# Squares by ACT from natural tiles, S5 operators on VectorE alone, tables turned in small steps

## Chip, cores and metric

One core of one Trainium2 chip runs the whole program. The metric is the device time of one execution in microseconds, the median of several runs.

## What is computed

A two-layer decoder trunk on x of 512 tokens by 2048 channels, float32. Layer 0 normalises x, multiplies it by one wide weight matrix (`ab_w_in`), and runs gated linear attention and forgetting attention side by side; layer 1 normalises, projects, and runs a diagonal complex state-space layer (S5), a GLU and an output projection. Cut to what the change touches:

```
def rms_norm(x, g):
    y = x * rsqrt(mean(x * x, axis=-1) + EPS)
    return y * g

def layer_ab(x, norm_g, w_in, ...):
    h = rms_norm(x, norm_g)
    g_q, g_k, g_v, g_lr, g_gate, f_q, f_k, f_v, f_f, f_gate = split(h @ w_in)
    ...

def s5_ssm(u, lam_re, lam_im, log_step, b_re, b_im, c_re, c_im, d):
    # groups of 16 channels share 64 complex states:
    # x_t = Lbar x_{t-1} + Bbar u_t ; y_t = Re(C x_t) + D u_t
```

S5 is computed in chunks of 8 tokens. Its operators depend on the parameters alone: powers of Lbar times C (`wc`), B with its factor (`wb`), and the products of the two, the taps (`KD`, with D on the diagonal). The kernel builds them while the first stages of layer 0 run.

## The kernel before

**Stages.** The first stages multiply the normalised x by columns of `ab_w_in`. `proj_x` and `proj_w` go over 16 tiles of 128 rows, two per chunk, so 8 chunks make a stage: one value stage (`gv0`, 512 columns), three gate stages (350, 350 and 348 columns, accumulators `g_a`), two transposed gate stages (`fg_a`, 512 columns each), then the q projection (`gq_a`) and the rest. For each chunk SP's queue loads the raw weights (`wload`, L147 and following, tile `wr`, three buffers), ACT casts them (`wh`, L166), DVE takes the remainder (`wl`, L167; four buffers of each, so two chunks), and PE runs 24 matmuls (L173 to L175: wh by the rounded x, wl by the rounded x, wh by x's remainder). Four accumulators per stage are evacuated at its end; the next stage reuses them.

**The first stage.** x comes transposed (`xT`, tiles `x`), is multiplied by the norm's gain on ACT (`hT_h`, L249), and DVE takes the remainder (`hT_l`, L250). `square` (L280 to L288) squares each tile on ACT into one buffer, and GpSimd adds it to `sq1`; `rstd_of_columns` sums the columns with four matmuls by a column of ones (`ps_r1`), and GpSimd's power gives `r1`, which the evacuation of the value stage needs (L617).

**The S5 work** is a generator (`s5_all`), of which the stages take a step per chunk through `paced`: one per chunk in the first stage, then three per four chunks. `s5_parameters` computes the powers on DVE (tiles `es..`, `em..`, `sn`, `cs`, `pri`, `bri`), in program order. `turn` transposes them on PE and copies them on ACT to the tables `tabc` (32 copies, two halves) and `tabb` (4), L465. `s5_operators` then makes 16 blocks. In block b SP loads `pd` (256 KB, L510, three buffers, two blocks ahead); GpSimd copies its first part to `wc` (L516), DVE multiplies (`wc`, L487), GpSimd multiplies (`s5t`, L487), DVE adds (L308), and GpSimd stores `wc` (L520) and makes `wby` and `wb` (L524, L525). Two steps later `taps` runs eight small matmuls (`k`, L534), ACT copies to one of two `kst` tiles (L536), DVE adds D on the diagonal (two stt on 128x16, L305), and GpSimd stores it (`KD`, L540). `lay_out_taps` copies KD to `MD` inside DRAM on SP's queue (L499) as soon as that KD has landed.

**Order.** Each engine and queue runs its own list in order. The tile scheduler sets these lists from program order, priorities (`high_priority` for weight casts and evacuations) and its own estimate; `keep_in_program_order` pins an instruction. `wr`, `pd` and `MD` all stand in SP's one list. All DMAs started by GpSimd stand in GpSimd's list between its arithmetic.

Of the kernel before, what the change touches and what calls it, by code (L numbers as in the profile page):

```python
# [8 lines left out]
F32 = mybir.dt.float32  # L9
# [30 lines left out]
def tile_trunk(  # L40
# [41 lines left out]
    G.memset(mhalf, -0.5)  # L82
    ones = const.tile([P, 1], F32, name="ones")
    G.memset(ones, 1.0)

# [191 lines left out]
    mix = []  # L277
    sq1 = t2("sq1")

    def square(k):  # L280

        xk = xt[k // 4][:, k % 4]
        if k == 0:
            tc.keep_in_program_order(A.activation(sq1, xk, AF.Square))
        else:
            junk = ev(f"junk{k}")
            tc.keep_in_program_order(A.activation(junk, xk, AF.Square))
            G.tensor_tensor(sq1, sq1, junk, op=ALU.add)  # L288

# [26 lines left out]
    dT = const.tile([P, 2, NB], F32, name="dT")  # L316
    dmask = const.tile([P, CI], F32, name="dmask")

    def s5_parameters(pp):
# [146 lines left out]

        yield
        for half in range(2):
            sl = slice(half * 4, half * 4 + 4)
            turn(f"tabc{half}", pri[:, 1 + half * 4:5 + half * 4], tc_.rearrange("p b y g n -> p n b y g")[:, sl], (1.0, 1.0), (-1.0, 1.0))  # L470
            yield
        turn("tabb", bri[:, 0:1], tb_.unsqueeze(1), (1.0, -1.0), (-1.0, -1.0))
        ts(bi_, bi_, -1.0, ALU.mult)
# [3 lines left out]
        V.tensor_copy(l8i.rearrange("p (b g) -> p b g", g=GB), tc_[:, :, 1, :, 7])  # L477
        tt(dmask, ident[:, 0:16], ident[:, 32:48], ALU.add)
        tt(dmask, dmask, ident[:, 64:80], ALU.add)
        tt(dmask, dmask, ident[:, 96:112], ALU.add)  # L480


    def s5_mul(eng, o, b, pd, y):
# [3 lines left out]
        return eng.tensor_tensor(o, t, c, op=ALU.mult)  # L487

# [13 lines left out]
    def s5_operators():  # L502
        with tc.tile_pool(name="pp", bufs=1) as pp:
# [4 lines left out]
            def load(b):  # L508
                pd = pp.tile([P, 4, GB, CI], F32, tag="pd", name=f"pd{b}", bufs=3)
                SP.dma_start(pd, s5_bc[:, b])  # L510
                return pd

            def operands(b, pd):
                tm = pp.tile([P, GB, T, CI], F32, tag="tm", name=f"s5t{b}", bufs=2)
# [9 lines left out]
                G.tensor_tensor(wy, pd[:, 2:], tb_[:, b].unsqueeze(3).to_broadcast([P, 2, GB, CI]), op=ALU.mult)  # L524
                G.tensor_tensor(wb, wy[:, 0].unsqueeze(2).to_broadcast([P, GB, 2, CI]), wy[:, 1].unsqueeze(2).to_broadcast([P, GB, 2, CI]), op=ALU.add)  # L525
                return wc, wb

            def taps(b, wc, wb):
                ks = kst[b % 2]
                ps = pst(f"k{b}")  # L530
                for hb in range(2):
                    for g in range(4):
                        gg = g * 2 + hb
                        PE.matmul(ps[g * 32:g * 32 + 32, hb * P:(hb + 1) * P], wb[:, gg].rearrange("p n c -> p (n c)"),  # L534
                                  wc[:, gg, 0:8].rearrange("p n c -> p (n c)"), start=True, stop=True)
                A.copy(ks[:, :, P:], ps[:, :256].rearrange("p (h n) -> p h n", h=2))  # L536
                for hb in range(2):
                    k0 = ks[:, hb, P:P + CI]
                    stt(k0, dmask, dT[:, hb, b:b + 1], k0, ALU.mult, ALU.add)
                G.dma_start(KD[b].rearrange("y (g n) -> g y n", g=4), ks.rearrange("p h n -> p (h n)"))  # L540

            pds, ops = [load(0), load(1)], {}
            yield
            yield
            for b in range(NB + 2):
                if b >= 2:
                    taps(b - 2, *ops.pop(b - 2))
                if b < NB:
                    ops[b] = operands(b, pds.pop(0))
                if b + 2 < NB:  # L550
                    pds.append(load(b + 2))
                yield
# [31 lines left out]

    def rstd_of_columns():
        nonlocal r1
        ps = pst("ps_r1")
        for i in range(NT):
            tc.keep_in_program_order(PE.matmul(ps[:, i:i + 1], sq1[:, i * P:(i + 1) * P], ones, start=True, stop=True))
        t = small("r1_s", 4)  # L590
        V.tensor_copy(t, ps[:, :NT])
        r1 = const.tile([P, NT], F32, name="r1")
        V.tensor_copy(r1, rstd_from(t, D, 4, "r1_p"))
        V.tensor_scalar(r1h, r1, 0.5, None, op0=ALU.mult)
# [25 lines left out]

    tc_ = tb_ = None

    def s5_all():
        nonlocal tc_, tb_
        with tc.tile_pool(name="tab", bufs=1) as tab:
            tc_ = tab.tile([P, NB, 2, GB, T], F32, name="tabc")
            tb_ = tab.tile([P, NB, 2, GB], F32, name="tabb")
            with tc.tile_pool(name="np", bufs=1) as pp:
                ordered[0] = True
# [4 lines left out]
    def first_hook():  # L634
# [758 lines left out]
```

## Time and profile before

| | |
|---|---|
| median of three runs | 1732.05 us (1731.59 to 1736.32) |
| the profiled execution | 1734.72 us, its span 1733.0 us |
| PE busy | 1677.7 us, 97% |
| DVE busy | 950.1 us, 55% |
| ACT busy | 637.4 us, 37% |
| POOL busy | 311.1 us, 18% |
| granted clock of PE | 0.987 of full speed |

PE is TensorE's matmuls, PEld its weight loads, DVE VectorE, ACT ScalarE, POOL GpSimd, SP the sync engine, which only starts DMAs. The shares are averages over the whole span; the change touches stages that take about a sixth of it.

### The profile page before, as it was taken

The numbers are of one execution on the slowest core, as the hardware profiler recorded it, in microseconds if no ns is written. First come the engines' busy times: TensorE is split into PE (matmuls) and PEld (weight loads), VectorE is DVE, ScalarE is ACT, GpSimd is POOL, SyncE is SP. The second block draws the span as 40 slices with busy tenths as digits, with TensorE's granted clock in tenths as the row PEclk, the third lists the DMA queues.
The fourth block names the chain that finished last, engine by engine and source line by source line (L and its number), as shares of the span: only waits on it lengthen the run. The fifth ranks groups of instructions, "written<-read, shape, count | busy, mean of one in ns | idle before, by whom it ended". The sixth has DMA issues, their size and how long they took to land.

```text
span 1733.0 us, 25458 instructions
## 1 busy us (share of the span) xinstructions
PE 1677.7 (97%) x9849; PEld 1380.0 (80%) x9849; DVE 950.1 (55%) x1686; ACT 637.4 (37%) x1186; POOL 311.1 (18%) x454
## 2 busy tenths in 40 slices
PE   7988979999999999999999999998999999999998
PEld 5988757788888888888888878786888788888886
DVE  8747874538543343355565775886762654443333
ACT  5352223625422362255343222223334433332223
POOL 5036643207100000010011122211112200020000
PEclk9998999999999999999999999999999999999999
DMA  5236776332223332342565899754679633363333
GB/s 198 84 109 211 250 218 205 101 96 86 74 65 96 95 93 79 124 162 79 135 188 170 189 233 222 211 155 136 204 222 281 179 118 98 97 217 96 96 96 128
DMA packets 151033, 255.36 MB, mean 147 GB/s; under 512 B 34872, under 2 KB 57416, under 8 KB 150784
## 3 DMA queue, kind: packets, MB, share of 16 engines
q1 hardware_dynamic: 99440, 163.80, 31.1%
q0 software_dynamic: 31488, 79.43, 16.2%
q10 hardware_dynamic: 19984, 10.52, 2.2%
q8 instruction: 77, 1.26, 0.3%
q14 instruction: 44, 0.36, 0.1%
HBM read 218.45 MB, written 43.53 MB: 151 GB/s over the span
## 4 chain that ended last, share of the span: by engine, by line
PE 77%; DMA 11%; issue 6%; DVE 4%; POOL 1%; ACT 1%; SPq 0%; ACTq 0%; POOLq 0%; DVEq 0%
PE gl_a L173 3%; PE gl_a L175 3%; PE gl_a L174 3%; PE cg_a L173 3%; PE co_a L174 3%; PE co_a L175 3%; PE cg_a L174 3%; PE co_a L173 3%; PE cg_a L175 3%; DMA wr<-in_ab_w_in_dram 3%; PE u_a L173 2%; PE u_a L175 2%; PE u_a L174 2%; PE fq_a L173 2%; PE fq_a L175 2%
## 5 line engine op out<-in xcount | busy, mean ns | idle before, releaser
L167 DVE TENSOR_TENSOR wl<-wr,wh 128x512 fp32r<-128x512 f32 (+2 forms) x560 | 397.6, 724 | 584.1 <-ACT wh L166 356.9
L166 ACT CAST wh<-wr 128x512 fp32r<-128x512 f32 (+2 forms) x560 | 337.5, 609 | 850.9 <-PE u_a L174 126.4
L173 PE MATMUL gl_a<-z_h,wh 128*128 128x512 f32 x256 | 100.3, 392 | 3.1 <-DVE gt L1229 3.1
L173 PE MATMUL cg_a<-h_h,wh 128*128 128x512 f32 x256 | 102.9, 402 | 0.0
L173 PE MATMUL u_a<-h_h,wh 128*128 128x512 f32 x256 | 101.0, 395 | 1.6 <-DVE ut L1111 1.6
L175 PE MATMUL u_a<-h_h,wl 128*128 128x512 f32 x256 | 100.1, 391 | 1.3 <-DVE wl L167 1.3
L174 PE MATMUL cg_a<-h_l,wh 128*128 128x512 f32 x256 | 100.6, 393 | 0.0
L175 PE MATMUL gl_a<-z_h,wl 128*128 128x512 f32 x256 | 100.3, 392 | 0.0
L174 PE MATMUL gl_a<-z_l,wh 128*128 128x512 f32 x256 | 100.2, 392 | 0.0
L175 PE MATMUL cg_a<-h_h,wl 128*128 128x512 f32 x256 | 100.2, 391 | 0.0
L174 PE MATMUL co_a<-wl,fh 128*128 128x512 f32 x256 | 99.7, 389 | 0.2 <-DVE wl L167 0.2
L174 PE MATMUL u_a<-h_l,wh 128*128 128x512 f32 x256 | 99.8, 390 | 0.0
L173 PE MATMUL co_a<-wh,fh 128*128 128x512 f32 x256 | 99.6, 389 | 0.0
L175 PE MATMUL co_a<-wh,fl 128*128 128x512 f32 x256 | 99.6, 389 | 0.0
L173 PE MATMUL g_a<-wh,hT_h 128*128 128x350 f32 (+1 forms) x192 | 65.5, 341 | 6.4 <-DVE mix L567 5.1
L174 PE MATMUL g_a<-wl,hT_h 128*128 128x350 f32 (+1 forms) x192 | 64.7, 337 | 3.7 <-DVE wl L167 3.7
L173 PE MATMUL fg_a<-hT_h,wh 128*128 128x512 f32 x128 | 52.8, 413 | 13.9 <-DVE gT L579 8.7
L175 PE MATMUL g_a<-wh,hT_l 128*128 128x350 f32 (+1 forms) x192 | 64.2, 334 | 0.0
L173 PEld LDWEIGHTS gl_a<-z_h,wh 128*128 128x128 f32 x256 | 48.4, 189 | 13.9 <-issue 3.5
L173 PEld LDWEIGHTS u_a<-h_h,wh 128*128 128x128 f32 x256 | 48.1, 188 | 12.3 <-issue 2.0
L175 PEld LDWEIGHTS u_a<-h_h,wl 128*128 128x128 f32 x256 | 48.0, 188 | 12.2 <-DVE wl L167 2.2
L173 PEld LDWEIGHTS cg_a<-h_h,wh 128*128 128x128 f32 x256 | 48.4, 189 | 11.3
(388 smaller groups left out, 3866.3 us busy)
## 6 DMA issues: line engine op xcount, KB each, us to landing
wr<-in_ab_w_in_dram SPq DMA_DIRECT2D x95, 512.0 KB
wr<-in_c_w_in_dram SPq DMA_DIRECT2D x64, 512.0 KB
wr<-in_ab_w_out_dram SPq DMA_DIRECT2D x32, 512.0 KB
wr<-in_glu_w_dram SPq DMA_DIRECT2D x32, 512.0 KB
wr<-in_c_w_out_dram SPq DMA_DIRECT2D x32, 512.0 KB
WcD<-wc POOLq DMA_DIRECT2D x16, 576.0 KB, 7.2
wcl<-WcD POOLq DMA_DIRECT2D x16, 576.0 KB, 6.6
MD<-KD SPq DMA_DIRECT2D x16, 512.0 KB
```

The source lines that it names most:

```text
L166: A.copy(h[:, :ncol], raw[:, k, :ncol])
L167: split[k].tensor_tensor(l[:, :ncol], raw[:, k, :ncol], f32(h[:, :ncol]), op=ALU.subtract)
L173: PE.matmul(ps, ah, bh, start=first, stop=False)
L174: PE.matmul(ps, ah, bl, start=False, stop=False)
L175: PE.matmul(ps, al, bh, start=False, stop=last)
```

## The change

1. The squares no longer come from the transposed tiles. `load_sq` loads x a second time, untransposed, as 16 tiles of 128 tokens by 512 channels (256 KB each, on SP's queue, three per chunk); ACT squares each with a sum along the row (`accum_out`). `rstd_first` adds the four sums of each token on DVE. GpSimd's 15 additions, the matmuls by ones and `rstd_of_columns` go.
2. `turn` yields after each transposed tile, so that the turning is 9 steps, not 3; the pace in the gate stages and the transposed gate stages becomes one step per chunk.
3. In `s5_operators` the arithmetic of GpSimd goes to DVE (`s5t`, `wby`, `wb`) and ACT (the copy to `wc`). `pd` is loaded by GpSimd's queue, with four buffers and three blocks ahead; `s5t` has one buffer.
4. D on the diagonal is prepared once for all blocks (`dk`), so that a block needs one addition on 128x2x16.

```
-    def square(k):
-        xk = xt[k // 4][:, k % 4]
...
-            tc.keep_in_program_order(A.activation(junk, xk, AF.Square))
-            G.tensor_tensor(sq1, sq1, junk, op=ALU.add)
+    def load_sq(n):
+        t = t2(f"xs{n}")
+        tc.keep_in_program_order(SP.dma_start(t, x2d[n // 4 * P:(n // 4 + 1) * P, n % 4 * 512:(n % 4 + 1) * 512]))
+        xsq.append((n, t))
+    def square():
+        n, t = xsq.pop(0)
+        A.activation(t, t, AF.Square, accum_out=ss1[:, n // 4, n % 4:n % 4 + 1])
...
                     for y, sg in enumerate((even, odd)):
                         A.activation(dst[hs, k, :, y], pv[y * 64:y * 64 + 64, k], AF.Copy, scale=sg[half])
+                yield
...
             def load(b):
-                pd = pp.tile([P, 4, GB, CI], F32, tag="pd", name=f"pd{b}", bufs=3)
-                SP.dma_start(pd, s5_bc[:, b])
+                pd = pp.tile([P, 4, GB, CI], F32, tag="pd", name=f"pd{b}", bufs=4)
+                G.dma_start(pd, s5_bc[:, b])
...
-                G.tensor_copy(wc[:, :, 0], pd[:, 0])
-                tc.keep_in_program_order(s5_mul(V, wc[:, :, 1:9], b, pd, 0))
-                s5_mul(G, tm, b, pd, 1)
+                A.copy(wc[:, :, 0], pd[:, 0])
+                tc.keep_in_program_order(s5_mul(wc[:, :, 1:9], b, pd, 0))
+                s5_mul(tm, b, pd, 1)
                 tt(wc[:, :, 1:9], wc[:, :, 1:9], tm, ALU.add)
...
-                G.tensor_tensor(wy, ...)
-                G.tensor_tensor(wb, ...)
+                V.tensor_tensor(wy, ...)
+                V.tensor_tensor(wb, ...)
...
-                for hb in range(2):
-                    k0 = ks[:, hb, P:P + CI]
-                    stt(k0, dmask, dT[:, hb, b:b + 1], k0, ALU.mult, ALU.add)
+                k0 = ks[:, :, P:P + CI]
+                tt(k0, k0, dk[:, :, b], ALU.add)
...
-            pds, ops = [load(0), load(1)], {}
+            pds, ops = [load(b) for b in range(3)], {}
...
+                if b + 3 < NB:
+                    pds.append(load(b + 3))
                 if b >= 2:
                     taps(b - 2, *ops.pop(b - 2))
...
+        while xsq:
+            square()
         for k in range(3 * n, min(3 * n + 3, KT)):
-            square(k)
+            load_sq(k)
         if n == 6:
-            rstd_of_columns()
+            rstd_first()
...
-    s5_steps = paced(s5, 3, 4)
+    s5_steps = paced(s5, 1)
```

The order on the queues, at three places. First SP's queue in the first stage, before (`wr_317` is the sixth weight chunk, `x_97` to `x_100` are quarters of the transposed x):

```order
L157 DMA wr_175<-in_ab_w_in_dram 128x2x512
L157 DMA wr_238<-in_ab_w_in_dram 128x2x512
L106 DMA x_99<-in_xT_dram 128x4x512
L157 DMA wr_317<-in_ab_w_in_dram 128x2x512
L157 DMA wr_401<-in_ab_w_in_dram 128x2x512
L106 DMA x_100<-in_xT_dram 128x4x512
L157 DMA wr_471<-in_ab_w_in_dram 128x2x512
L157 DMA wr_671<-in_ab_w_in_dram 128x2x350
```

and after the change, where `wr_314` is the sixth chunk and `xs` are the new tiles for the squares:

```order
L155 DMA wr_172<-in_ab_w_in_dram 128x2x512
L155 DMA wr_235<-in_ab_w_in_dram 128x2x512
L104 DMA x_97<-in_xT_dram 128x4x512
L104 DMA x_98<-in_xT_dram 128x4x512
L282 DMA xs_182<-in_x_dram 128x512
L282 DMA xs_184<-in_x_dram 128x512
L282 DMA xs_186<-in_x_dram 128x512
L282 DMA xs_248<-in_x_dram 128x512
L282 DMA xs_250<-in_x_dram 128x512
L282 DMA xs_252<-in_x_dram 128x512
L155 DMA wr_314<-in_ab_w_in_dram 128x2x512
L282 DMA xs_327<-in_x_dram 128x512
```

Six loads of `xs` and the last quarter of x now stand ahead of the sixth weight chunk.

Second, ACT at the end of the second gate stage (`tg_2398` is the tanh that evacuates its accumulators, the casts of 348 columns belong to the third), before:

```order
L166 CAST wh_0_1347<-wr_1345 128x350
L166 CAST wh_1_1351<-wr_1345 128x350
L166 CAST wh_0_1423<-wr_1421 128x348
L166 CAST wh_1_1427<-wr_1421 128x348
L565 ACTIVATE tg_2398_1405<-g_a_1052,r1h 128x350
L565 ACTIVATE tg_2398_1408<-g_a_1053,r1h 128x350
L565 ACTIVATE tg_2398_1411<-g_a_1054,r1h 128x350
L166 CAST wh_0_1457<-wr_1455 128x348
L166 CAST wh_1_1461<-wr_1455 128x348
L565 ACTIVATE tg_2398_1414<-g_a_1055,r1h 128x350
L536 COPY kst_1175<-k_1379 128x2x128
```

and after the change:

```order
L164 CAST wh_1_1322<-wr_1316 128x350
L164 CAST wh_0_1368<-wr_1366 128x348
L164 CAST wh_1_1372<-wr_1366 128x348
L514 COPY wc_1403<-pd_1310 128x8x16
L514 COPY wc_1450<-pd_1312 128x8x16
L562 ACTIVATE tg_2398_1350<-g_a_1026,r1h 128x350
L514 COPY wc_1509<-pd_1314 128x8x16
L562 ACTIVATE tg_2398_1353<-g_a_1027,r1h 128x350
L562 ACTIVATE tg_2398_1356<-g_a_1028,r1h 128x350
L164 CAST wh_0_1415<-wr_1413 128x348
L164 CAST wh_1_1419<-wr_1413 128x348
L562 ACTIVATE tg_2398_1359<-g_a_1029,r1h 128x350
```

Three copies from `pd` to `wc` now stand before and between the first tanh, and so ahead of the casts of the third stage's next chunks.

Third, SP's queue in the transposed gate stages, before:

```order
L157 DMA wr_2019<-in_ab_w_in_dram 128x2x512
L510 DMA pd_1847<-in_s_bc_dram 128x512
L499 DMA MD<-KD 1024x1x128
L157 DMA wr_2079<-in_ab_w_in_dram 128x2x512
L510 DMA pd_1957<-in_s_bc_dram 128x512
L499 DMA MD<-KD 1024x1x128
L157 DMA wr_2113<-in_ab_w_in_dram 128x2x512
L157 DMA wr_2173<-in_ab_w_in_dram 128x2x512
L510 DMA pd_2017<-in_s_bc_dram 128x512
L499 DMA MD<-KD 1024x1x128
L157 DMA wr_2233<-in_ab_w_in_dram 128x2x512
```

and after the change:

```order
L497 DMA MD<-KD 1024x1x128
L155 DMA wr_1830<-in_ab_w_in_dram 128x2x512
L497 DMA MD<-KD 1024x1x128
L155 DMA wr_1889<-in_ab_w_in_dram 128x2x512
L497 DMA MD<-KD 1024x1x128
L155 DMA wr_1948<-in_ab_w_in_dram 128x2x512
L497 DMA MD<-KD 1024x1x128
L155 DMA wr_2007<-in_ab_w_in_dram 128x2x512
L497 DMA MD<-KD 1024x1x128
L155 DMA wr_2066<-in_ab_w_in_dram 128x2x512
L155 DMA wr_2125<-in_ab_w_in_dram 128x2x512
```

`pd` has left the queue; MD and the weight loads alternate.

## Rows read from the trace of the kernel before

**Rows 1.** The page, busy times of the whole execution.

```profile
PE 1677.7 (97%) x9849; PEld 1380.0 (80%) x9849; DVE 950.1 (55%) x1686; ACT 637.4 (37%) x1186; POOL 311.1 (18%) x454
```

**Rows 2.** Table by stage: busy us of PE, PEld, DVE, ACT, POOL; clock, DMA share, GB/s.

```profile
133.00:180.00 47.00, 41.44 (x309) 37.52 (x308) 38.02 (x43) 10.96 (x27) 29.93 (x32) 0.89 0.71 222
180.00:294.00 114.00, 100.10 (x534) 77.84 (x534) 75.41 (x87) 27.75 (x53) 55.80 (x85) 0.96 0.75 234
294.00:1733.00 1439.00, 1417.30 (x8412) 1160.69 (x8410) 747.20 (x1336) 531.98 (x977) 179.92 (x293) 1.00 0.48 139
```

**Rows 3.** Timeline of ACT (start us, us): casts, a gate stage and a 512-column stage.

```profile
81.70 0.97 ACT L166 CAST wh<-wr 128x350 fp32r<-128x350 f32 x2 [2.87 <-PE g_a L175]
...
287.29 1.14 ACT L166 CAST wh<-wr 128x512 fp32r<-128x512 f32 x2 [4.33 <-PE fg_a L175]
```

**Rows 4.** PE matmuls of four stages (min/median/max ns, first and last start); timeline at 133.

```profile
L173 PE MATMUL gv_a<-wh,hT_h x128: 387/389/796, 5.1 to 440.8; 128*128 128x512 f32 x128
...
L173 PE MATMUL g_a<-wh,hT_h x192: 316/323/629, 62.4 to 177.7; 128*128 128x350 f32 x128, 128*128 128x348 f32 x64
...
L173 PE MATMUL fg_a<-hT_h,wh x128: 389/389/767, 179.8 to 292.5; 128*128 128x512 f32 x128
...
L173 PE MATMUL gq_a<-hT_h,wh x64: 389/389/499, 293.6 to 342.2; 128*128 128x512 f32 x64
...
133.17 0.32 PE L175 MATMUL g_a<-wh,hT_l 128*128 128x350 f32 x1
```

**Rows 5.** Table by stretch as in rows 2, first stage.

```profile
10.00:20.00 10.00, 8.95 (x39) 7.08 (x39) 8.02 (x12) 8.97 (x17) 6.43 (x5) 1.00 0.91 329
...
40.00:50.00 10.00, 10.00 (x37) 8.00 (x37) 10.00 (x43) 3.01 (x5) 1.83 (x1) 0.81 0.13 37
```

**Rows 6.** DVE's timeline near 12 us, then costly groups of DVE and POOL before 62.

```profile
9.59 1.41 DVE L250 SCALAR_TENSOR_TENSOR hT_l<-x,cols,hT_h 128x512 fp32r<-128x512 f32 x2 [0.60 <-ACT hT_h L249]
...
14.21 3.26 DVE L250 SCALAR_TENSOR_TENSOR hT_l<-x,cols,hT_h 128x512 fp32r<-128x512 f32 x2 [1.52 <-ACT hT_h L249]
...
L250 DVE SCALAR_TENSOR_TENSOR hT_l<-x,cols,hT_h 128x512 fp32r<-128x512 f32 x16 | 14.6, 925 | 3.8 <-ACT hT_h L249 3.8
...
L308 DVE TENSOR_TENSOR emp<-emp,emr 128x64 f32<-128x64 f32 x7 | 1.5, 216 | 0.0
...
L288 POOL TENSOR_TENSOR sq<-sq,junk 128x512 f32<-128x512 f32 x15 | 22.7, 1516 | 20.3 <-ACT junk L287 19.5
```

**Rows 7.** Timeline of ACT between the first two gate stages.

```profile
99.22 3.28 ACT L465 ACTIVATE tabc<-tabc 64x128 f32<-64x128 f32 x8
```

**Rows 8.** Waits from 103 to 294 us: total, times, longest us.

```profile
ACT wh L166 <- DMA wr<-in_ab_w_in_dram: 61.2, 11, 11.0
...
POOL wby L524 <- DMA pd<-in_s_bc_dram: 42.7, 9, 9.8
...
SPq L499 <- DMA KD<-kst: 60.9, 9, 11.5
```

**Rows 9.** Timelines of SP's queue, POOL and ACT near 220 us.

```profile
214.28 5.57 SPq L157 DMA_DIRECT2D wr<-in_ab_w_in_dram  x1
219.94 0.52 SPq L510 DMA_DIRECT2D pd<-in_s_bc_dram  x1
...
226.46 1.15 POOL L524 TENSOR_TENSOR wby<-pd,tabb 128x256 f32<-128x256 f32 x1 [9.79 <-DMA pd<-in_s_bc_dram]
...
225.78 1.14 ACT L166 CAST wh<-wr 128x512 fp32r<-128x512 f32 x2 [10.23 <-DMA wr<-in_ab_w_in_dram]
```

**Rows 10.** DVE's products of pd; KD's issue and landing; POOL's loads of x.

```profile
L487 DVE TENSOR_TENSOR wc<-tabc,pd x16: 1210/1213/2957, 117.7 to 259.7; 128x1024 f32<-128x1024 f32 x16
...
L540 POOL DMA_DIRECT2D KD<-kst x16: 722/757/777, 139.9 to 277.8; - x16
...
DMA to landing us min/median/max: 6.1/7.0/9.6
...
x<-in_x_dram POOLq DMA_DIRECT2D x16, 256.0 KB, 4.0
```

More of the change, by code (lines that the diff above doesn't have):

```diff
@@ L82, in tile_trunk @@
     G.memset(mhalf, -0.5)
-    ones = const.tile([P, 1], F32, name="ones")
-    G.memset(ones, 1.0)
     idle = ev("idle")
@@ L277, in tile_trunk @@
     mix = []
-    sq1 = t2("sq1")
-    def square(k):
-        xk = xt[k // 4][:, k % 4]
[L283 to L286, printed above, removed]
-            tc.keep_in_program_order(A.activation(junk, xk, AF.Square))
-            G.tensor_tensor(sq1, sq1, junk, op=ALU.add)
+    ss1 = const.tile([P, NT, 4], F32, name="ss1")
+    xsq = []
+    def load_sq(n):
[5 more added lines that the diff above has]
+        A.activation(t, t, AF.Square, accum_out=ss1[:, n // 4, n % 4:n % 4 + 1])
     fb = const.tile([8, 1], F32, name="fb")
@@ L316, in tile_trunk @@
     dT = const.tile([P, 2, NB], F32, name="dT")
-    dmask = const.tile([P, CI], F32, name="dmask")
     def s5_parameters(pp):
@@ L469, in s5_parameters @@
             sl = slice(half * 4, half * 4 + 4)
-            turn(f"tabc{half}", pri[:, 1 + half * 4:5 + half * 4], tc_.rearrange("p b y g n -> p n b y g")[:, sl], (1.0, 1.0), (-1.0, 1.0))
-            yield
-        turn("tabb", bri[:, 0:1], tb_.unsqueeze(1), (1.0, -1.0), (-1.0, -1.0))
+            yield from turn(f"tabc{half}", pri[:, 1 + half * 4:5 + half * 4], tc_.rearrange("p b y g n -> p n b y g")[:, sl], (1.0, 1.0), (-1.0, 1.0))
+        yield from turn("tabb", bri[:, 0:1], tb_.unsqueeze(1), (1.0, -1.0), (-1.0, -1.0))
         ts(bi_, bi_, -1.0, ALU.mult)
@@ L477, in s5_parameters, with s5_mul @@
         V.tensor_copy(l8i.rearrange("p (b g) -> p b g", g=GB), tc_[:, :, 1, :, 7])
[L478 to L483, printed above, removed]
+        dmask = nt("dmask", CI)
+        V.tensor_reduce(dmask, ident.rearrange("p (j c) -> p c j", j=4)[:, :CI], axis=mybir.AxisListType.X, op=ALU.add)
+        tt(dk, dmask.unsqueeze(1).unsqueeze(1).to_broadcast([P, 2, NB, CI]), dT.unsqueeze(3).to_broadcast([P, 2, NB, CI]), ALU.mult)
+    def s5_mul(o, b, pd, y):
         t = tc_[:, b, y].unsqueeze(3).to_broadcast([P, GB, T, CI])
         c = pd[:, y].unsqueeze(2).to_broadcast([P, GB, T, CI])
-        return eng.tensor_tensor(o, t, c, op=ALU.mult)
+        return V.tensor_tensor(o, t, c, op=ALU.mult)
     WcD = dr.tile([NB, P, GB * 9 * CI], F32, name="WcD")
@@ L508, in load @@
             def load(b):
-                pd = pp.tile([P, 4, GB, CI], F32, tag="pd", name=f"pd{b}", bufs=3)
-                SP.dma_start(pd, s5_bc[:, b])
+                pd = pp.tile([P, 4, GB, CI], F32, tag="pd", name=f"pd{b}", bufs=4)
+                G.dma_start(pd, s5_bc[:, b])
                 return pd
             def operands(b, pd):
-                tm = pp.tile([P, GB, T, CI], F32, tag="tm", name=f"s5t{b}", bufs=2)
+                tm = pp.tile([P, GB, T, CI], F32, tag="tm", name=f"s5t{b}")
                 wc = pp.tile([P, GB, 9, CI], F32, tag="wc", name=f"wc{b}", bufs=3)
-                G.tensor_copy(wc[:, :, 0], pd[:, 0])
-                tc.keep_in_program_order(s5_mul(V, wc[:, :, 1:9], b, pd, 0))
-                s5_mul(G, tm, b, pd, 1)
+                A.copy(wc[:, :, 0], pd[:, 0])
+                tc.keep_in_program_order(s5_mul(wc[:, :, 1:9], b, pd, 0))
+                s5_mul(tm, b, pd, 1)
                 tt(wc[:, :, 1:9], wc[:, :, 1:9], tm, ALU.add)
@@ L523, in operands @@
                 wy = pp.tile([P, 2, GB, CI], F32, tag="wby", name=f"wby_{b}", bufs=2)
-                G.tensor_tensor(wy, pd[:, 2:], tb_[:, b].unsqueeze(3).to_broadcast([P, 2, GB, CI]), op=ALU.mult)
-                G.tensor_tensor(wb, wy[:, 0].unsqueeze(2).to_broadcast([P, GB, 2, CI]), wy[:, 1].unsqueeze(2).to_broadcast([P, GB, 2, CI]), op=ALU.add)
+                V.tensor_tensor(wy, pd[:, 2:], tb_[:, b].unsqueeze(3).to_broadcast([P, 2, GB, CI]), op=ALU.mult)
+                V.tensor_tensor(wb, wy[:, 0].unsqueeze(2).to_broadcast([P, GB, 2, CI]), wy[:, 1].unsqueeze(2).to_broadcast([P, GB, 2, CI]), op=ALU.add)
                 return wc, wb
@@ L549, in s5_operators @@
                     ops[b] = operands(b, pds.pop(0))
-                if b + 2 < NB:
-                    pds.append(load(b + 2))
                 yield
@@ L583, in evac_gateT, with rstd_first @@
         return f
-    def rstd_of_columns():
+    def rstd_first():
         nonlocal r1
[L587 to L593, printed above, removed]
+        r1 = token_rstd(ss1, "r1")
         V.tensor_scalar(r1h, r1, 0.5, None, op0=ALU.mult)
@@ L619, in evac_gv @@
         return f
-    tc_ = tb_ = None
+    tc_ = tb_ = dk = None
     def s5_all():
-        nonlocal tc_, tb_
+        nonlocal tc_, tb_, dk
         with tc.tile_pool(name="tab", bufs=1) as tab:
@@ L627, in s5_all @@
             tb_ = tab.tile([P, NB, 2, GB], F32, name="tabb")
+            dk = tab.tile([P, 2, NB, CI], F32, name="dk")
             with tc.tile_pool(name="np", bufs=1) as pp:
```

## The prediction

> **What bounds the kernel now.** I read the page's busy times first [rows 1]: TensorE (PE) is busy 97% of the span, so little can be won, and the question is where. The table by stage answers it [rows 2]: from 294 us to the end PE is busy 1417.3 of 1439 us at a granted clock of 1.00, before that it is not, and the clock is lower. The whole change lies before 294 us, and behind it the orders of the engines are the same, so what the first stages win or lose is carried to the end.
>
> How much can be lost there follows from pitches. ACT casts a chunk when PE has done another, and where only PE holds it, busy and idle add up to PE's pitch: 0.97 + 2.87 = 3.84 us in a gate stage, 1.14 + 4.33 = 5.47 us in a 512-column stage [rows 3]. The first PE instruction of each stage [rows 4] gives what each took: the first value stage (8 chunks) 57.3 us against 43.8, the three gate stages (24) 117.4 against 92.2, the two transposed gate stages (16) 113.8 against 87.5. The last matmul of the second gate stage [rows 4] puts its end at 133.5, so gate stages 1 and 2 lost 9.7 us and the third 15.6. Lost in all: 13.5 + 9.7 + 15.6 + 26.3 = 65 us. That is the ceiling.
>
> Why each is lost. **First stage:** PE is behind, and VectorE (DVE) is the engine without a gap: from 40 to 50 us it is busy 10 of 10 us, while PE's clock is granted at 0.81 on average, a mix of the 2.4 and 1.2 GHz levels after PE's waits just before [rows 5]. DVE is slow because GpSimd adds squares: two hT_l take 1.41 us before GpSimd starts and 3.26 during its first additions [rows 6]. **Gate stages 1 and 2:** ScalarE (ACT) runs the copies of the turned tables in runs between the tanh of the evacuation (one of the four in [rows 7]), and PE, whose accumulators wait for those, idles. **Third gate stage and after:** ACT waits 61.2 us for weights (wr), GpSimd 42.7 us for pd, SP's queue 60.9 us for KD to land [rows 8]. The timelines show a ring: SP lays out MD only when a KD has landed, and the weight load behind it goes at 214.28, the pd behind that at 219.94; GpSimd stands 9.79 us until that pd is there, at 226.46, and only then issues its next KD, for which the next MD, weights and pd wait; ACT meanwhile waits 10.23 us for the weights [rows 9].
>
> **The change, part by part.**
> *A, squares.* Removed: 15 additions on GpSimd, 22.7 us [rows 6], and the four small ps_r1 matmuls. Against the undisturbed 0.70 the 16 hT_l of 925 ns hold 3.6 us too much, and wl and the small steps are stretched alike. The 16 squares stay on ACT. Added: 16 loads of 256 KB on SP's queue, 4.2 MB or 12.7 us at the 329 GB/s of the second 10 us, into a stage whose DMA share falls to 0.13 [rows 5]. Six of them and 2 MB of x now stand ahead of the sixth weight chunk; from 13 us on that is 3.6 MB, 11 us, so it lands near 26 to 28 us, and an unstalled PE needs it at 33. In the new order DVE runs 36 small steps in one piece before the wl of that chunk, 36 of 216 ns [rows 6], less than 8 us; I charge 3 us of PE waits to it and 1.5 to the late r1 (two last loads, two squares, the reduction, GpSimd's power), and 1.6 remain from the first two chunks. 13.5 - 6.1 gives **-7 us**.
> *B, tables.* The 16 copies of a half still stand together on ACT, but between two casts, away from the tanh: 16 x 0.41 + 0.97 = 7.5 us [rows 7] against two chunks of 7.68 until the cast is needed, with its wl about 0.9 us late. Twice that is 1.8 in place of 9.7: **-8 us**.
> *C, third gate stage.* New: in the order of ACT two copies wc<-pd stand ahead of the first tanh of the second gate stage, and on DVE the first s5t stands ahead of one wl. pd can only start when LbD has landed and kst is cleared. pd has no row on GpSimd's queue; the nearest are x, a load of the same 256 KB there, with 4.0 us, and KD, a store of 256 KB, with up to 9.6 [rows 10]; a pd already there would cost nothing. I take x's 4 and count the queue in the new order from the start of the last table: a wait of 2.3 us, plus 1.2 at the lower clock, 3.5; the ends are 0 and 9. DVE's part of a block becomes 3 x 1.21 [rows 10], 2 x 0.42 for wy and wb (256 columns, estimated between 0.22 for 64 and 1.21 for 1024), 0.22 for the tap [rows 6]: 4.7 us. Five blocks (23.5), 15 wl and four mix (some 0.5 each) stand ahead of the last wl of this stage, 33 us against 30.7 - 2 of PE: 4.4 late. The two kst buffers need a KD landed two chunks later: 3 us to its issue and 7.0 to landing (6.1 to 9.6 [rows 10]) against 2 x 4.4 here, for the few blocks of this stage about 3. So 30.7 + 10.9 against 46.3: **-5 us**. GpSimd's arithmetic goes, and with it DVE's stretched rows.
> *D, transposed gates.* pd no longer passes SP, so KD follows its block. KD is issued about 3 us after its matmuls, lands 8 later, MD and wr follow, wr lands 10 later (214.28 to the cast at 225.78 is 11.5 [rows 9]), cast and wl take 2.5: 23.5 us, and in the new order five chunks, 27.4 us, lie between. It fits narrowly. DVE needs 4.7 + 1.3 = 6.0 us per chunk while blocks remain (ten chunks), 0.5 above 5.47: 5.3; 7 more for late transfers and the two evacuations. 87.5 + 12.3 against 113.8: **-14 us**.
> The wc copies that move to ACT, where casts fill 1.14 of 5.47 us, I cost at nothing while pd is there first; if it is not, see the slower rival. GpSimd's three issues per block, pd's now among them, take some 0.75 each of 6 us.
>
> For the move of pd the Trainium skill speaks against a gain: DMA: Bandwidth & Descriptors, "Issuing engines are not separate DMA queues", says all queues run on the same 16 engines and that another issuer only saves issue time. By it D would lose its 14 us and the sum be 20, or 1712, close to the first rival below. The rows disagree: pd's issue takes 0.52 us on SP, but it stood behind a weight load that took 5.57 to go and an MD that waited for KD, and GpSimd paid 9.79 us for it [rows 9].
>
> **Sum:** 7 + 8 + 5 + 14 = 34 us. The profiled execution took 1734.7 us and gives 1700.7; the median of the three runs is 2.7 us lower, 1732.05, and gives **1698 us**.
>
> **Rivals.**
> *The 16 DMA engines become the bound.* From 133 to 294 us they are busy 0.71 x 47 + 0.75 x 114 = 119 us [rows 2]. The same transfers in my 141 us mean a share of 0.84; the best 10 us hold 0.91 [rows 5], the two stages now 0.71 and 0.75. If 0.77 is the most that holds for long, C and D end at 154 us in place of 160: with A and B a gain of 21, **1711 us**. Against it: much of today's idle share is the ring. Chance 0.22.
> *A or B fails* (the sixth weight chunk comes late behind the loads of squares; or the 16 copies in one piece stall PE as they do now, so that the small steps are none): 7 or 8 us less, **1706**. Chance 0.05.
> *All fits better:* DVE and KD hide behind PE, gain 46 to 55, **1682**. Chance 0.07.
> *Slower: ACT inherits the wait for pd.* GpSimd waits 4.7 us for pd on average (42.7 over 9 waits) and feeds no cast; ACT does. If each of 16 blocks held ACT for 7 us, 3.3 above the slack of 5.47 - 1.14 - 0.65, C and D would end at 118 (pitches) + 23 + 53 = 194 us in place of 160: with A and B **1751 us**. It decides from 6 us per block. For it: pd on GpSimd's queue stands behind WcD and KD, which wait for DVE. Against it: pd is issued three blocks, some 16 us, ahead. Chance 0.04.
> The Trainium skill bears on this rival: SBUF — State Buffer, "Summary: rules for kernel authors", advises the SP or ACT queue for a load under DVE work, since descriptors made on GpSimd starve in some of DVE's modes. KD's issue, 722 to 777 ns over 16 [rows 10], shows no such starving beside DVE's work.
> *No change* (half of each term, and the rest eaten by such waits): 1732, chance 0.02.
>
> **How the numbers follow.** Forecast (gain 24 to 46) 0.60, and the rivals as above. A measurement here tells 0.3%, 5.2 us, from no change. Faster 0.92 (forecast, DMA bound, A or B, all fits, less 0.02 for what I have not seen), same 0.03, slower 0.05. The range takes in the DMA rival to a gain of 12 and most of the better case: 1684 to 1720.
>
> **What would show it.** gate stages starting near 55 us, the third near 118 and the first q projection (gq_a) near 260; no GpSimd arithmetic from 10 to 250 us except one power; hT_l at 0.70 to 0.75 us throughout; no GpSimd wait for pd, SP's wait for KD well under 60.9 us, ACT's for wr well under 61.2; DVE near full and DMA share above 0.8 from 120 to 230 us; ACT and DVE waiting once for pd near 118 us. Wrong: ACT's wait for wr still above 50 us (DMA bound, or the ring through MD lives on without pd), or ACT waiting for pd block by block.

## The result, and the profile after

The changed kernel takes 1707.53 us (median of four runs, 1705.76 to 1711.91), the kernel before 1734.18 beside it: a ratio of 0.9835 with a 95% interval of 0.9805 to 0.9865. It is faster by 26.7 us where 34 were forecast, and lies in the range. The profiled execution has a span of 1704.2 us, against 1733.0.

The page's busy times of the changed kernel, for [rows 1]:

```profile
PE 1667.2 (98%) x9841; PEld 1374.0 (81%) x9841; DVE 920.9 (54%) x1717; ACT 643.0 (38%) x1218; POOL 224.0 (13%) x390
```

Its table by stretch and stage, with the columns of [rows 2]:

```profile
10.00:20.00 10.00, 10.00 (x45) 8.28 (x45) 8.06 (x18) 5.90 (x10) 0.00 (x0) 1.00 1.05 390
40.00:50.00 10.00, 10.00 (x46) 8.09 (x44) 4.00 (x19) 4.58 (x12) 1.05 (x1) 1.00 0.61 199
50.00:114.30 64.30, 64.03 (x398) 62.71 (x397) 30.02 (x79) 34.20 (x79) 4.06 (x7) 1.00 0.35 107
114.30:155.60 41.30, 35.66 (x290) 32.54 (x289) 34.16 (x57) 13.14 (x33) 9.51 (x16) 0.99 0.77 242
155.60:265.10 109.50, 101.73 (x549) 79.28 (x549) 72.51 (x111) 29.96 (x61) 31.15 (x76) 0.94 0.79 253
265.10:1704.00 1438.90, 1417.31 (x8415) 1161.39 (x8412) 747.90 (x1337) 532.68 (x978) 173.96 (x276) 1.00 0.48 139
```

The last row is the check that all of it lies ahead: 1438.9 us, where [rows 2] has 1439.0. The first row (10 to 20 us) now has PE without a gap. The third gate stage and the transposed gates are the two with idle PE. Their idle time, span less PE's busy time, is 5.6 and 7.8 us. The third gate stage of the kernel before, cut at the same landmarks, shows as much idle time (5.5 us), but a lower granted clock:

```profile
133.50:179.80 46.30, 40.76 (x304) 37.05 (x304) 37.48 (x43) 10.31 (x25) 29.23 (x31) 0.89 0.70 222
```

The first matmuls of the four stages, for [rows 4]:

```profile
L171 PE MATMUL gv_a<-wh,hT_h x128: 389/389/796, 5.1 to 412.3; 128*128 128x512 f32 x128
...
L171 PE MATMUL g_a<-wh,hT_h x192: 316/322/431, 50.0 to 150.7; 128*128 128x350 f32 x128, 128*128 128x348 f32 x64
...
L171 PE MATMUL fg_a<-hT_h,wh x128: 389/389/796, 155.6 to 264.0; 128*128 128x512 f32 x128
...
L171 PE MATMUL gq_a<-hT_h,wh x64: 389/389/499, 265.1 to 313.7; 128*128 128x512 f32 x64
```

The gate stages start at 50.0, the transposed gates at 155.6, the q projection at 265.1, 28.5 us earlier than before.

The waits from 100 to 265.1 us (total, times, longest), for [rows 8], first of the engines (a selection):

```profile
ACT wh L164 <- DMA wr<-in_ab_w_in_dram: 37.3, 9, 9.5
...
ACT wc L514 <- DMA WcD<-wc: 14.8, 5, 4.2
...
ACT wc L514 <- DMA pd<-in_s_bc_dram: 2.7, 3, 1.9
...
DVE s5t L485 <- DMA pd<-in_s_bc_dram: 1.8, 1, 1.8
```

and of SP's queue:

```profile
SPq L497 <- DMA KD<-kst: 9.8, 4, 8.0
```

SP's wait for KD fell from 60.9 to 9.8 us. GpSimd's 42.7 us for pd are gone, since it no longer reads pd; ACT and VectorE wait 4.5 us for it in its place. ACT still waits 37.3 us for weights, where it was 61.2, and the experiments below are mostly about that row.

### The profile page after: what moved, and what is told of

It reads as the page before. It is cut to its first block, busy times and chain, and to the rows that moved or that the text cites. A ratio compares the mean times of both kernels' runs of the same rounds, so it can differ in the third digit from the quotient of the medians.

```text
span 1704.2 us, 25406 instructions
## 1 busy us (share of the span) xinstructions
PE 1667.2 (98%) x9841; PEld 1374.0 (81%) x9841; DVE 920.9 (54%) x1717; ACT 643.0 (38%) x1218; POOL 224.0 (13%) x390
## 4 chain that ended last, share of the span: by engine, by line
PE 84%; issue 6%; DMA 5%; DVE 2%; POOL 1%; ACT 1%; POOLq 0%; ACTq 0%; DVEq 0%; SPq 0%
PE gl_a L171 3%; PE gl_a L173 3%; PE gl_a L172 3%; PE u_a L171 3%; PE u_a L173 3%; PE u_a L172 3%; PE co_a L172 3%; PE co_a L173 3%; PE co_a L171 3%; PE cg_a L171 3%; PE cg_a L172 3%; PE cg_a L173 3%; PE fq_a L171 2%; PE fq_a L173 2%; PE oa_a L171 2%
## 5 line engine op out<-in xcount | busy, mean ns | idle before, releaser
L165 DVE TENSOR_TENSOR wl<-wr,wh 128x512 fp32r<-128x512 f32 (+2 forms) x560 | 373.7, 681 | 593.9 <-ACT wh L164 357.0
L171 PEld LDWEIGHTS gl_a<-z_h,wh 128*128 128x128 f32 x256 | 48.5, 189 | 14.3 <-issue 4.3
L171 PEld LDWEIGHTS u_a<-h_h,wh 128*128 128x128 f32 x256 | 48.0, 188 | 12.3 <-issue 2.0
```

Source lines behind the costliest of these rows:

```text
L165: split[k].tensor_tensor(l[:, :ncol], raw[:, k, :ncol], f32(h[:, :ncol]), op=ALU.subtract)
L171: PE.matmul(ps, ah, bh, start=first, stop=False)
```

## The experiments

Each run is read by its stages, from the first matmul of one to that of the next (gate stages 1 and 2: to the end of the last matmul with 350 columns). These landmarks come from the one profiled execution of each kernel, and repeat within some 1.6 us where the code is the same (the first stage of the kernels with the new squares takes 44.0 to 45.6). The whole time repeats less well: in layer 1, whose code no run here changes, the stretch from the first u_a to the first cg_a matmul took 194.4 us before, 193.4 after the change and up to 201.4 in the other runs. A gain at the q projection is therefore not yet a gain of the median, and both are given where both were measured.

| kernel | first stage | gates 1, 2 | gate 3 | transposed gates | q starts at |
|---|---|---|---|---|---|
| before | 57.3 | 71.1 | 46.3 | 113.8 | 293.6 |
| before + squares | 45.0 | 71.9 | 45.5 | 112.0 | 279.4 |
| before + turning, pace 1 | 56.4 | 64.5 | 49.2 | 127.0 | 302.1 |
| before + arithmetic moved | 57.6 | 70.0 | 44.5 | 117.9 | 295.1 |
| before, MD later | 57.2 | 71.3 | 43.1 | 101.7 | 278.5 |
| **changed** | 44.9 | 64.3 | 41.3 | 109.5 | 265.1 |
| changed, pd on SP | 44.0 | 64.3 | 41.2 | 105.7 | 260.3 |
| changed, arithmetic on GpSimd | 44.5 | 64.3 | 47.8 | 112.0 | 273.8 |
| changed, MD later | 44.6 | 64.3 | 39.7 | 97.0 | 250.8 |
| changed, MD on GpSimd | 44.4 | 64.3 | 40.1 | 122.6 | 276.5 |
| changed, MD on GpSimd, behind | 45.6 | 64.3 | 41.2 | 100.8 | 257.0 |
| changed, MD on SP, behind | 44.7 | 64.3 | 41.6 | 108.2 | 264.0 |
| MD later + copies of x on SP | 44.4 | 64.3 | 39.5 | 115.9 | 269.2 |
| changed, MD later, blocks pinned | 45.2 | 64.3 | 33.3 | 98.2 | 246.2 |

Six of the kernels were run once only, and are read by their stages; no run has the fourth part, D on the diagonal, by itself. The single times are 1706.62 us (pd on SP), 1723.11 (arithmetic on GpSimd), 1721.73 and 1702.55 (MD on GpSimd, and behind), 1708.33 (MD on SP, behind) and 1726.50 (copies of x).

### One part at a time, in the kernel before

**Squares alone.** The edit is the first piece of the diff, with `load_sq`, `square`, `rstd_first` and the hook.

> The kernel before with the squares alone (loads of untransposed x, ACT's sums along the row, no additions on GpSimd); the S5 work as before. Theory (GpSimd's additions slowed VectorE in the first stage, and nothing else of the change acts there): the gate stages start near 50 us as in the changed kernel, not at 62.4, hT_l falls to about 0.7 us, and the 12 us are kept to the end: about 1722. Rival (the gain of the first stage is given back, because the blocks then meet the same ring earlier): the gate stages start near 50, but the q projection starts less than 6 us earlier than 293.6, and the time is above 1728.

1727.61 us, ratio 0.995 (0.9932 to 0.9968). The first stage takes 45.0 us, as in the changed kernel, and the q projection starts 14.2 us earlier: the gain is kept up to there, and the rival falls. The median time is 9.1 us below that of the kernel before beside it (1736.71), where 12 were expected. The profiled execution has the lowest of the ten times (1723.61), so its landmarks flatter the part somewhat. The ring lives on beside it (SP waits 59.1 us for KD).

**Turning and pace alone.**

```
-            turn(f"tabc{half}", ...)
-            yield
+            yield from turn(f"tabc{half}", ...)
...
-    s5_steps = paced(s5, 3, 4)
+    s5_steps = paced(s5, 1)
```

> The kernel before with the turning in nine steps and the pace of one step per chunk alone. Theory (ACT's runs of copies delayed the tanh at the ends of the stages): gate stages 1 and 2 take about 64 us in place of 71, and the time falls by about 7 to 1727. Rival (a faster pace only drives the ring of KD, MD and weights harder): the first two gate stages are shorter, but the third and the transposed gate stages together are longer by as much, and the time stays within 3 us of the kernel before.

1747.27 us, ratio 1.0052 (1.0032 to 1.0072): slower. The first two gate stages fall to 64.5 us, as the theory said, but the third and the transposed gates take 16.1 us more. The rival was right that they get longer, and the loss is larger than it said. Its reason does not show in the waits, though: SP waits less for KD than before (49.7 us for 60.9) and ACT less for weights (36.7 for 61.2). What grew is ACT's wait for one of the two kst buffers, that is, for an older KD to land; casts stand behind that copy on ACT's list. Before, from 100 to 300 us:

```profile
ACT kst L536 <- DMA KD<-kst: 15.1, 5, 3.9
```

and with the turning in steps and the pace of one:

```profile
ACT kst L536 <- DMA KD<-kst: 45.8, 11, 10.1
```

In the changed kernel it is 3.1 us. Alone, the part does not pay. The edit has two halves, and no run separates the steps of the turning from the pace.

**Arithmetic alone**, VectorE's and ACT's part of `operands`, with pd as before (the last run, after those below):

> The kernel before with the S5 operators' arithmetic moved to VectorE and ACT alone (pd stays on SP with three buffers and two blocks ahead, squares, turning and pace as before). Theory formed from the runs so far (the link of the ring that mattered is KD's place in GpSimd's list behind arithmetic that waits for pd): SP's wait for KD falls below 20 us from 60.9, third gate stage and transposed gates together fall from 160.4 us to 150 or less, the time by 8 to 14. Rival (it needs pd on its own queue as well, as the prediction had it): KD waits stay over 40 us, gain under 4.

1741.79 us, ratio 1.0036 (1.002 to 1.0051): my theory fell. The waits of this kernel from 100 to 300 us, VectorE's for pd:

```profile
DVE wby L524 <- DMA pd<-in_s_bc_dram: 38.4, 9, 5.3
```

and SP's queue for KD:

```profile
SPq L499 <- DMA KD<-kst: 70.1, 11, 8.4
```

What GpSimd waited for pd, VectorE now waits, nearly microsecond for microsecond (42.7 and 38.4), and VectorE feeds the weights too. In this kernel, the arithmetic without an earlier pd is worth nothing.

### Undoing one part of the changed kernel

```
-                G.dma_start(pd, s5_bc[:, b])
+                SP.dma_start(pd, s5_bc[:, b])
```

> The changed kernel with pd loaded by SP's queue again (four buffers and three blocks ahead stay, the arithmetic stays on VectorE and ACT). Theory of the prediction (what helped from the third gate stage on is that pd no longer passes SP, where it stood behind MD and weights): the ring is back, SP waits for KD more than 30 us in place of 9.8, and the q projection starts after 274 us in place of 265.1. Rival (what helped is that the arithmetic left GpSimd; pd three blocks ahead is early enough on either queue): the q projection starts within 3 us of 265.

The q projection starts at 260.3, SP waits 10.3 us for KD: no ring, and the theory of the prediction falls. The rival's 3 us are missed too, on the good side: the start is 4.8 us earlier than in the changed kernel. Once the load goes out three blocks ahead into four buffers, GpSimd's queue is no better for pd than SP's. ACT waits 23.5 us for pd in this run, and yet no stage is longer than in the changed kernel.

The arithmetic back on GpSimd (`G.tensor_copy`, `s5_mul(G, ...)`, `G.tensor_tensor` for wby and wb, two s5t buffers):

> The changed kernel with the S5 operators' arithmetic back on GpSimd and VectorE as before (s5t with two buffers), pd on GpSimd's queue three blocks ahead. Theory (pd's own queue was what helped): the q projection starts within 4 us of 265.1. Rival (the arithmetic on GpSimd stood between the transfers that its list starts and slowed VectorE's rows, so that it was the bound at a pace of one step per chunk): VectorE's products take well over 1.21 us on average, the transposed gates take over 118 us, the q projection starts after 274.

273.8, 8.7 us later, 6.5 of them in the third gate stage; SP waits 22.4 us for KD and ACT 54.4 for weights. Where the arithmetic stands matters, given an early pd. VectorE's products explain a part of it at most:

```profile
L485 DVE TENSOR_TENSOR wc<-tabc,pd 128x1024 f32<-128x1024 f32 x16 | 22.7, 1420 | 1.6 <-DMA pd<-in_s_bc_dram 1.6
```

Their mean is 1420 ns for 1218 in the changed kernel, 3.2 us over all 16. Their median is 1213 ns, as in [rows 10]: a few are slow, not all.

### The copies of the taps (MD)

`lay_out_taps` stands in the program much later, in the forgetting attention's k projection. The scheduler pulls the copies forward on SP's list to the place where each KD may be ready. One line keeps them back, in the kernel before and in the changed one (the first copy then starts at 457.1 us in place of 147.9, and at 429.1 in place of 137.9, some 300 us later and not the 200 that the expectations name):

```
-            SP.dma_start(MD[b]..., ...)
+            tc.keep_in_program_order(SP.dma_start(MD[b]..., ...))
```

> The kernel before with the copies of the taps (MD) pinned where the program has them, in the k projection of the forgetting attention some 200 us later, and nothing else changed; only SP's list differs. Theory of the ring (the wait of SP for KD, 60.9 us, held weights and pd): SP's wait for KD is gone before 294 us, ACT's wait for weights falls below 25 us from 61.2, and third gate stage and transposed gate stages together fall by 15 to 25 us: 1710 to 1719. Rival (the 16 DMA engines or GpSimd's arithmetic are the bound): less than 8 us, above 1726.

> The changed kernel with the copies of the taps (MD) pinned where the program has them, some 200 us later; only SP's list differs. Theory (what the transposed gates still lose, 22 us, is weights that land 10 to 14 us after their issue because the DMA engines are full at a share of 0.86, and MD is a good part of that load): the share falls below 0.75, ACT's wait for weights from 120 to 265 us falls from 37 to under 15, the transposed gates take about 95 us, and the time falls by 12 to 18: about 1692. Rival 1 (VectorE's 6 us per chunk bound it): share falls, VectorE is busy near 100%, the transposed gates take over 103 us, gain under 6. Rival 2 (ACT's copies to wc, which wait for the store WcD, hold the casts): ACT waits 12.9 us for WcD as now, gain under 6.

In the kernel before, this line alone brings 15.1 us at the q projection (293.6 to 278.5). The median time falls by 10.2 us, to 1726.55 (ratio 0.9946, 0.9923 to 0.9969), short of the 1710 to 1719 that were expected; here too the profiled execution has the lowest of ten times (1718.42). No wait for weights is left there, and GpSimd's wait for pd falls to 8.2 us. In the changed kernel it brings 14.3 us (265.1 to 250.8; 1697.02 us, ratio to before 0.9771, 0.9733 to 0.9809). The transposed gates of that version:

```profile
153.80:250.80 97.00, 96.25 (x548) 75.31 (x548) 72.17 (x111) 31.32 (x61) 30.63 (x76) 1.00 0.68 207
```

PE is busy 96.25 of 97.0 us at a clock of 1.00, VectorE 72. So VectorE is no bound, and ACT's wait for WcD (24.9 us in this run, more than in the changed kernel) costs nothing. Most of what PE does in the 9.5 us above the pitch of 87.5 is the taps, per block one group of eight small matmuls, which stand as 16 records in the trace, here in the changed kernel's timeline:

```profile
176.15 0.39 PE L173 MATMUL fg_a<-hT_h,wl 128*128 128x512 f32 x1
176.54 0.64 PE L532 MATMUL k<-wc,wb 128*32 128x128 f32 x16
177.11 0.50 PE L171 MATMUL fg_a<-hT_h,wh 128*128 128x512 f32 x1
```

From the last matmul ahead to the first behind it is 0.96 us, where 0.23 is the step: some 0.7 us per block, and ten blocks (160 of the 548 records) fall into this stage: 7 us.

Three causes for the late weights remained: MD's bytes, SP's waits for KD, or the copies on SP's queue by themselves. MD on GpSimd's queue keeps the bytes in the stage:

```
-            SP.dma_start(MD[b]..., ...)
+            G.dma_start(MD[b]..., ...)
...
                     taps(b - 2, *ops.pop(b - 2))
+                if b >= 4:
+                    next(laid)
```

> The changed kernel with MD copied by GpSimd's queue, two blocks behind the store of KD, in the same stages; SP's list is then weights alone. It keeps MD's bytes in the stage and takes its place in SP's list away. Theory of the bytes (full DMA engines make the weights late): DMA share near 0.8, ACT's waits for weights from 120 to 265 us over 25 us, the transposed gates 105 to 110 us. Theory of the list (SP's wait for KD and MD's turn ahead of the weights made them late): ACT's waits for weights under 10 us, the transposed gates 97 to 100 us as with MD moved away, the q projection near 252.

This try made a ring of its own and settles little:

```profile
POOL MD L497 <- DMA KD<-kst: 87.0, 15, 9.8
```

GpSimd stood for KD. Still, ACT had no wait for weights at all. So once more, with the copies pinned and begun at block 5 (`b >= 5`, `keep_in_program_order`); and, in another kernel, the same on SP's queue:

> MD on GpSimd's queue once more, now pinned five blocks behind the operators (three behind the store of KD), so that GpSimd no longer stands for KD, which took 87 us of its list in the first try. SP's list is weights alone, MD's bytes stay in the stage. Theory of the bytes: DMA share 0.78 to 0.85, ACT waits over 20 us for weights, the transposed gates take over 105 us. Theory of SP's list: no wait for weights, the transposed gates 97 to 101 us, the q projection at 251 to 255.

> MD on SP's queue between the weights as in the changed kernel, but each copy pinned three blocks behind its KD, so that SP has no KD to wait for; bytes and number of starts on SP as in the changed kernel. If SP's waits for KD (9.8 us there) made the weights late: no wait for KD, ACT's waits for weights fall from 37 us to under 12, the transposed gates take under 101 us. If the bytes, or MD's transfer ahead of the weights on the same queue, did it: the transposed gates take 105 to 110 us as in the changed kernel.

On GpSimd's queue the transposed gates take 100.8 us, with no wait for weights and the DMA engines fuller than in this stage of any other run:

```profile
156.20:210.00 53.80, 52.51 (x323) 40.06 (x324) 48.49 (x73) 15.31 (x36) 24.39 (x32) 0.97 0.97 317
```

A share of 0.97 at 317 GB/s, and the weights are in time. The theory of the bytes falls. One thing besides the queue changed, however: on SP's queue a copy of 512 KB goes out as 1024 packets of 512 bytes, on GpSimd's as 128 of 4 KB and some tiny ones. Over the transposed gates SP's queue (hardware) and GpSimd's (software) moved, in packets, MB and share of the engines, in the changed kernel

```profile
q1 hardware_dynamic: 19505, 17.01, 49.4%
q0 software_dynamic: 5186, 10.64, 28.9%
```

and with MD on GpSimd, behind,

```profile
q0 software_dynamic: 9404, 19.09, 59.3%
q1 hardware_dynamic: 4611, 8.89, 27.0%
```

Whether it is the other queue or the fewer packets that freed the weights, no run here separates. On SP's queue the pinning moved nothing, since SP's list is ahead of the blocks: the same places, still 15.1 us of waiting for KD, 108.2 us. That run is inconclusive. The last one takes the wait away and leaves the copies:

```
+            tc.keep_in_program_order(SP.dma_start(MX[b]..., <the same shape, from x>))
...
+                if b >= 5:
+                    next(dummy)
```

> The version with MD pinned 200 us later, and in the third gate stage and the transposed gates 16 extra copies of the same shape from x to a scratch in DRAM on SP's queue, between the weights where the changed kernel has MD; they depend on nothing, so SP never waits for KD. If SP's waits for KD made the weights late: ACT waits under 12 us for weights and the transposed gates take 97 to 101 us although the bytes and the starts on SP are back. If MD's transfer on the same queue ahead of the weights does it by itself: ACT's waits for weights over 20 us and the transposed gates 104 to 110 us.

SP's waits for KD are gone, and the transposed gates take 115.9 us, more than the 104 to 110 that were expected; the weights are as late as ever. ACT's wait from 100 to 300 us:

```profile
ACT wh L164 <- DMA wr<-in_ab_w_in_dram: 43.2, 10, 12.7
```

and a piece of the timeline of SP's queue:

```profile
193.11 3.88 SPq L506 DMA_DIRECT2D MX<-in_x_dram  x1
...
216.09 12.38 SPq L506 DMA_DIRECT2D MX<-in_x_dram  x3
228.57 5.38 SPq L155 DMA_DIRECT2D wr<-in_ab_w_in_dram  x3
```

So it is the copies from DRAM to DRAM between the weights on SP's queue, by themselves. Three of them held SP's list for 12.38 us, and behind them stood weights that ACT then waited 12.70 us for. Those three are an exception, with a median of 0.81 us over the 16. What is slow as a rule is the start of the weight load behind a copy. The starts of weights on SP in the transposed gates (min/median/max ns), in the changed kernel:

```profile
L155 SPq DMA_DIRECT2D wr<-in_ab_w_in_dram x18: 367/4846/9217, 153.5 to 260.6; - x18
```

and with MD later:

```profile
L155 SPq DMA_DIRECT2D wr<-in_ab_w_in_dram x16: 367/368/368, 157.1 to 246.4; - x16
```

With MD on GpSimd, behind, they are 367/368/368 too; with the copies of x, 367/3438/10343. A weight load that takes 0.37 us to start alone takes 3 to 10 with such a copy ahead of it, and SP's list stands meanwhile. What in the copy causes it, its packets or its way from DRAM to DRAM, no run here separates.

### A version that beats both

MD later, and the block's work pinned, with its first block one step later:

```
-                A.copy(wc[:, :, 0], pd[:, 0])
+                tc.keep_in_program_order(A.copy(wc[:, :, 0], pd[:, 0]))
...
             yield
             yield
+            yield
             for b in range(NB + 2):
```

(and the same pin for the second product of pd, wby and wb; the first had it)

> The version with MD pinned 200 us later, and in it the copy to wc, both products of pd, wby and wb pinned to program order and the first block one step later, so that nothing of a block stands ahead of the tanh, the sums and the weights' remainders at the end of the second gate stage. Theory (waiting for pd there, on ACT and VectorE, costs the 3.5 us that the prediction charged): TensorE goes from the second to the third gate stage with under 1 us of idle, the q projection starts at 247 to 248 in place of 250.8. Rival (the wait only moves: the first block is later, and the end of the stage and the third stage lose as much elsewhere): 250 to 253.

1693.59 us, ratio to before 0.9759 (0.9731 to 0.9786), 246.2 at the q projection: 18.9 us earlier than the changed kernel. Against the version with MD later alone (1697.02) the medians are not clear of each other; the 4.6 us between those two are read at the q projection. PE goes from the second to the third gate stage without a gap:

```profile
114.36 0.32 PE L173 MATMUL g_a<-wh,hT_l 128*128 128x350 f32 x1
114.52 0.32 PE L171 MATMUL g_a<-wh,hT_h 128*128 128x348 f32 x1
```

and from the third to the transposed gates likewise (147.86 to 148.02). The third stage falls by 6.4 us and the transposed gates rise by 1.2, as some taps move there. The gain, 4.6 us, is more than the 3 that were expected, because the boundary behind the third stage gains too.

## Why the prediction came out as it did

By stage the change brought 12.4 + 6.8 + 5.0 + 4.3 = 28.5 us, where 7 + 8 + 5 + 14 = 34 stood in the sum. Two terms were mis-sized, in opposite directions, so that the sum came out nearer than its parts; one term was right by luck, and one reason was wrong. Of the landmarks named, the gate stages start at 50.0 (for 55), the third at 115.0 (118), the q projection at 265.1 (260); from 10 us to the masks at 242.60 GpSimd computes one power and clears kst, nothing else.

*A, squares: 12.4 us, not 7.* The cause was right: alone, the part gives the same 45 us. What failed is the 6.1 us of new and remaining waits that I charged; the stage has 1.1 us over its pitch. The sixth weight chunk was not waited for: the one wait for weights in this stage is 0.45 us, at 9.77 us, long before it. hT_l fell to 747 ns:

```profile
L248 DVE SCALAR_TENSOR_TENSOR hT_l<-x,cols,hT_h 128x512 fp32r<-128x512 f32 x16 | 11.8, 747 | 3.3 <-ACT hT_h L247 3.3
```

And the small steps that I multiplied by 216 ns follow each other faster than they last:

```profile
28.25 0.22 DVE L304 SCALAR_TENSOR_TENSOR emr<-emk,emx 128x64 f32<-128x64 f32 x1
28.39 0.22 DVE L304 SCALAR_TENSOR_TENSOR rr<-kq,rr 128x64 f32<-128x64 f32 x1
28.52 0.22 DVE L304 SCALAR_TENSOR_TENSOR emr<-emk,emr 128x64 f32<-128x64 f32 x1
```

0.22 us each, but a start every 0.13: 36 of them are under 5 us, not 8.

*B, tables: 6.8 us, not 8.* Right, in cause and size; 2.9 us remain over the pitch, for 1.8 forecast. That the same edit with its pace makes the kernel before slower (16.1 us in the later stages) I had not seen: I priced the terms as if they added, but at the faster pace ACT in that kernel waits 45.8 us for kst buffers, and 3.1 at the same pace in the changed one.

*C, third gate stage: 5.0 us, as forecast, by luck.* PE's idle time did not change (46.30 - 40.76 = 5.5 us before, 41.30 - 35.66 = 5.6 after). All that the stage gained is PE's busy time, 5.1 us at a granted clock of 0.99 in place of 0.89, and the term named no such gain; which of the parts raised the clock here, no run isolates. Nor is the time over the pitch what was charged (10.9 us of waits): of the 10.6 us measured, 5.0 are work of PE (35.66 us busy for the pitch of 30.7), most of it the taps of six blocks, which I had left out of the pitch; 5.6 are idle. The head-of-line wait for pd at the boundary is there (ACT 2.7 us, VectorE 1.8). The pinned version, with MD later, leaves under 0.2 us of idle PE in the stage, where MD later alone leaves 4.0, so work of the blocks cost PE more than that wait, at both ends of the stage. The 4.4 us of late VectorE was not: at the end ACT waited 6.7 us for weights that an MD stood ahead of.

*D, transposed gates: 4.3 us, not 14.* Here the step that failed is "pd no longer passes SP, so KD follows its block". KD does follow now, and SP's wait for it is 9.8 us. But not by pd's queue: on SP again it is as good. The runs point to pd's three blocks of lead together with the arithmetic off GpSimd: with the arithmetic alone SP waits 70.1 us for KD, with the lead and the arithmetic on GpSimd 22.4, with both and pd on SP 10.3 (the first of these kernels also differs in pace and squares; the lead alone, in the kernel before, was not run). And the weights were late for another reason than the ring: MD copies between them on SP's queue, 12.5 us of this stage by the run without them. Of these, 7.0 are idle time of PE (7.8 for 0.8) and 5.5 are the same matmuls taking longer (101.73 us busy for 96.25) at a granted clock of 0.94 in place of 1.00. My 23.5 us for the way from a block to its weights had the links, but took MD as something that waits for KD on SP, not as something that makes the weight load behind it slow to start.

The remainder was mis-made as well: I expected 5.3 us of VectorE and 7 of others over the pitch, 12.3. It is 22.0: 9.5 that remain without MD, mostly taps on PE, and 12.5 around MD. I had left the taps out of the pitch, so the ceiling of 65 was too high by them, here and in the third gate stage. VectorE's 5.3 does not show: with MD later the stage has 0.8 us of idle PE in all.

*The rivals.* "The 16 DMA engines become the bound" named nearly the right time, 1711, for a reason that the runs deny: at a share of 0.97 the weights come. The slower rival, ACT inheriting the waits for pd, did not come: 2.7 us in all; in the arithmetic alone, where pd is late and the time goes up, VectorE inherits them (38.4 us for wby) and ACT little (7.6).

*The Trainium skill's rule* (DMA: Bandwidth & Descriptors, "Issuing engines are not separate DMA queues") would have left D at nothing. For pd the runs agree with it: its queue made no gain. For MD they do not: the copies on GpSimd's queue in place of SP's take 7.4 to 8.7 us from the stage (108.2 with the same pinning on SP, 109.5 in the changed kernel, to 100.8). The Trainium skill's section allows another issuer a saving of issue time alone and calls that usually small; here the start of a weight load took 4.85 us at the median with MD on SP's queue and 0.37 without it. (The copies also went out in fewer packets there, so the queue by itself is not shown to be the cause.) The Trainium skill's advice against loads on GpSimd under VectorE's work (SBUF — State Buffer, "Summary: rules for kernel authors") was not followed, at no cost that shows here: KD's starts stay at 722 to 747 ns. Whether VectorE ran in one of the modes that the advice is about, no run here shows.

## What to carry to other kernels

Look where the scheduler puts a transfer that nobody needs soon: one pinned line was worth 15 us in the kernel before and 14 in the changed one at the start of the q projection (10 in the median time of the kernel before), half as much as the whole change. Read a queue as a list with transfers in it, not only with waits, look at how long each start on it takes, and try copies like MD's off the queue that feeds the critical loads. Before adding up the parts of a change, ask which part raises a rate that another part must bear. And split each stage into PE's idle time, its work and its clock before crediting a gain to a wait.

## What the hardware did that was not expected

A DMA share of 0.97 (317 GB/s over 54 us) did not delay the weights, while copies of 512 KB on the weights' own queue, at a share of 0.73 over the stage, did, though none of them had a KD to wait for. The start of a weight load on SP's queue took 4.85 us at the median in the transposed gates with MD between the weights, and 0.37 without. The copies went out in packets of 512 bytes from SP's queue and of 4 KB from GpSimd's. VectorE's small operations overlap: 0.22 us long, 0.13 apart, so that their durations, added up, overstate the time they take.
